# Attention in a gated block: sinks as a 129th score column, scaled queries, another order of transposes, stores and value loads

## The chip, the core and the metric

The kernel runs on one core of a Trainium2 chip. The metric is the device time of one execution in microseconds (us). Five engines work in parallel, each through its own instructions in their written order: TensorE (PE, with its weight loads PEld), VectorE (DVE), ScalarE (ACT), GpSimd (POOL) and SyncE (SP), which here issues all the DMAs.

## The reference

For 2048 positions of 1024 channels the block takes an RMS norm h, multiplies it by one wide weight (7680 columns), and feeds a convolution branch and an attention branch, which gates merge:

```python
proj = einsum("bsd,de->bse", h, w_in)          # glu_in, conv_gate, q, k, v, attn_gate, merge_logits
c = silu(layernorm(conv31(a * sigmoid(b)) + b_dw))
y_conv = (c * silu(conv_gate)) @ w_conv_out
# attention: 16 query heads, 4 key heads, head 64, window 128, rope on q and k
scores = where(mask, q k^T * 64 ** -0.5, -1e30)
m = maximum(max(scores), sink)
p = exp(scores - m)
probs = p / (sum(p) + exp(sink - m))
y_attn = ((probs v) * silu(attn_gate)) @ w_attn_out
merged = sigmoid(g_conv) * y_conv + sigmoid(g_attn) * y_attn
out = rmsnorm(x + merged @ w_out)
```

## The kernel before

Two sweeps of 1024 positions each run the same program. Every large product is made of three matmuls (high by high, high by low, low by high), since each operand is split into a rounded high half and what is left, its low half. Names begin `whi_` and `wlo_` for the halves of weights; in the first sweep POOL computes the low halves (L254) and SP stores them (L285), in the second sweep SP loads them again (L271). A projection (`project`, L297) is 48 matmuls of 512 columns into two of three PSUM banks "mm".

The order on PE is the order in which the program is written, and that comes from a planner, the class `Line`: it adds up PE's time (`spend`), and hands out the steps of side chains when they are due. `late` holds chains with a due time (`after`, `start`), `bg` the convolution's operations one per `every` us, `soon` one operation per step. The other engines' instructions are put in order ahead of time by dependences, estimated times and a priority (`tc.high_priority`).

The convolution is 31 taps for each of eight channel groups, each tap one pass of DVE over 1024 columns (L518). Attention runs beside the projections of the gates (`ag`, `cg`, `ma`, `mc`). It has 32 units a sweep, one per key head and block of 128 positions, ATT_EVERY = 13.8 us apart. A unit (`attention`, L720) is a chain of three steps with the pauses LAT between them:

- the scores `sc`, eight matmuls into two PSUM banks (L735); ACT copies and DVE masks them into the tile `ss` (L745, L748); DVE takes the maximum (L752), scales it and compares it with the negated sink (L753), and forms sink minus maximum (L755); ACT takes its exponential (L756) and those of the four heads with their sums (L758); DVE adds the sink's term (L760) and inverts (L761); ACT scales the rows (L763).
- four transposes of `ss` into one bank `tpp` (L768); ACT and DVE split it into `pt` (L775, L776), POOL selects from that `pc` (L780); the gate `ga` is loaded into `ss` (L771).
- six matmuls into the bank `ov` (L791); ACT and DVE add its two halves into `ss` (L797, L798), DVE multiplies by `ga` (L799), ACT and DVE split the product (L801, L802), and SP stores it to `d_a` (L804).

`sc`, `tpp` and `ov` share three PSUM banks, the pool "tp", in turn. Queries and keys of the next unit are loaded from DRAM (`qk`, L711, L715) when a unit begins, value tiles (`va`, `vb`, `vm`) per key head, eight units at once, when the last unit of a head has issued its product (`load_v`, L676). ACT changes its table of functions between the exponentials and the gates' functions (ACT_TABLE_LOAD). Gates are stored from their evacuation (L561), queries when two of a head's parts are split (L622). When all 32 units are stored, the output is loaded again as `aT` (L897) for the product `ya`.

## Time and profile before

| what | value |
|---|---|
| time, median of 3 runs (lowest, highest) | 2062.93 us (2062.31, 2063.85) |
| the profiled execution, time of its own | 2065.01 us |
| span from its first to its last instruction | 2063.3 us |
| mean granted TensorE clock in it | 0.991 |
| attention, first to last score matmul | 210.3 to 1698.3 us, in two sweeps |
| first and last load of `aT` in the first sweep | 645.9, 714.06 us |
| first `ya` matmul of the first and of the second sweep | 766.4, 1795.4 us |
| mean of one: ACT's Exp (L758), scaling (L763), copy of ov (L797), gate (L560) | 392, 393, 368, 600 ns |

The profile is of one execution. Its page has the busy time of each engine, the chain of work that ended last and the costliest groups of instructions by line; other views give the waits (which engine and line stood idle for whom, in all, how often, the longest), the timeline, and the busy time with the granted clock in chosen windows. A line such as L758 is a line of the kernel before.

### The profile page before, as it was taken

How to read it: one execution, taken by the hardware profiler on the slowest of the kernel's cores; microseconds unless marked ns; L12 is line 12 of the kernel's file. 1: busy time of each engine (PE TensorE's matmuls, PEld its weight loads, DVE VectorE, ACT ScalarE, POOL GpSimd, SP SyncE). 2: the span in 40 equal slices, each digit the busy share in tenths (PEclk: the TensorE clock that was granted, in tenths of full speed). 3: DMA queues.
4: the chain of work that ended last, by engine and by line, in shares of the span. 5: the costliest groups of instructions: out<-in, count | busy, mean ns of one | idle time of the engine just before them, and what ended most of it. 6: DMA issues, size and time to landing. Idle time of an engine off the chain costs nothing.

```text
span 2063.3 us, 27786 instructions
## 1 busy us (share of the span) xinstructions
PE 2001.2 (97%) x9264; PEld 1660.7 (80%) x9264; DVE 1330.4 (64%) x1930; ACT 1014.6 (49%) x2263; POOL 417.3 (20%) x398
## 2 busy tenths in 40 slices
PE   8999999999999999999999999999989999999998
PEld 7888788787887878888888778877878788888887
DVE  7998769888995266123766848589878934441224
ACT  8322576677657453124513125766666675621222
POOL 1454233233323322340001121111011110000200
PEclk9999999999999999999999999999999999999999
DMA  8656646546467857346646555565565668574432
GB/s 308 204 167 197 206 152 191 179 159 182 158 175 226 261 197 240 134 151 215 224 150 204 163 168 169 160 178 188 162 185 175 178 219 275 166 244 148 146 119 82
DMA packets 302015, 382.02 MB, mean 185 GB/s; under 512 B 29232, under 2 KB 160176, under 8 KB 301872
## 3 DMA queue, kind: packets, MB, share of 16 engines
q1 hardware_dynamic: 301872, 380.25, 58.1%
q8 instruction: 74, 1.21, 0.2%
q14 instruction: 69, 0.57, 0.1%
HBM read 252.20 MB, written 127.93 MB: 184 GB/s over the span
## 4 chain that ended last, share of the span: by engine, by line
PE 56%; DVE 20%; ACT 8%; DMA 3%; issue 2%; SPq 1%; POOL 0%; ACTq 0%; DVEq 0%; POOLq 0%
DVE acc L518 12%; PE o L1105 8%; PE mm_ya L292 8%; PE mm_yc L292 8%; PE mm_mc L292 7%; PE mm_ma L292 6%; PE mm_ga L292 4%; PE mm_gb L292 3%; PE mm_q_b L292 2%; PE mm_q_a L292 2%; ACT ss L758 2%; PE mm_cg L292 2%; DVE ss L798 1%; DVE st L752 1%; ACT L758 1%
## 5 line engine op out<-in xcount | busy, mean ns | idle before, releaser
L518 DVE SCALAR_TENSOR_TENSOR acc<-glu,par,acc 128x1024 f32<-128x1024 f32 x464 | 595.4, 1283 | 4.2
L780 POOL TENSOR_SCALAR_AFFINE_SELECT pc<-pt 64x512 fp32r<-64x512 f32 x128 | 83.6, 653 | 552.9 <-ACT pt L775 522.1
L1105 PE MATMUL o<-wo,mT 128*128 128x512 f32 x768 | 174.8, 389 | 0.0
L1105 PEld LDWEIGHTS o<-wo,mT 128*128 128x128 f32 x768 | 144.1, 188 | 30.0
L292 PE MATMUL mm_ma<-hT,whi_ma 128*128 128x512 f32 x512 | 162.7, 399 | 0.0
L292 PE MATMUL mm_cg<-hT,whi_cg 128*128 128x512 f32 x512 | 161.8, 397 | 0.0
L292 PE MATMUL mm_mc<-hT,whi_mc 128*128 128x512 f32 x512 | 158.4, 391 | 1.6 <-ACT mc L560 1.6
L292 PE MATMUL mm_ag<-hT,whi_ag 128*128 128x512 f32 x512 | 159.8, 393 | 0.0
L292 PE MATMUL mm_ya<-aT,whi_ya 128*128 128x512 f32 x512 | 157.7, 389 | 0.0
L292 PE MATMUL mm_yc<-uT,whi_yc 128*128 128x512 f32 x512 | 157.5, 389 | 0.0
L758 ACT ACT_TABLE_LOAD x57 | 73.1, 1283 | 142.0 <-DVE st L753 142.0
L292 PE MATMUL mm_ga<-hT,whi_ga 128*128 128x512 f32 x448 | 142.8, 400 | 0.0
L292 PE MATMUL mm_gb<-hT,whi_gb 128*128 128x512 f32 x448 | 139.9, 393 | 0.0
L292 PEld LDWEIGHTS mm_mc<-hT,whi_mc 128*128 128x128 f32 x512 | 95.3, 188 | 21.4 <-ACT mc L560 2.0
L292 PEld LDWEIGHTS mm_yc<-uT,whi_yc 128*128 128x128 f32 x512 | 96.1, 188 | 19.9
L292 PEld LDWEIGHTS mm_ya<-aT,whi_ya 128*128 128x128 f32 x512 | 96.0, 188 | 19.9
L292 PEld LDWEIGHTS mm_ma<-hT,whi_ma 128*128 128x128 f32 x512 | 94.8, 192 | 17.7
L798 DVE TENSOR_TENSOR ss<-ov,ss 64x256 f32<-64x256 f32 x128 | 53.7, 419 | 85.9 <-ACT ss L797 84.2
L292 PEld LDWEIGHTS mm_cg<-hT,whi_cg 128*128 128x128 f32 x512 | 94.0, 191 | 17.3
L292 PEld LDWEIGHTS mm_ag<-hT,whi_ag 128*128 128x128 f32 x512 | 93.4, 188 | 17.6
L292 PE MATMUL mm_ma<-hT,wlo_ma 128*128 128x512 f32 x256 | 101.7, 397 | 4.5 <-DMA wlo_ma<-d_lo 4.5
L292 PE MATMUL mm_cg<-hT,wlo_cg 128*128 128x512 f32 x256 | 101.2, 395 | 4.1 <-DMA wlo_cg<-d_lo 4.1
(450 smaller groups left out, 4350.8 us busy)
## 6 DMA issues: line engine op xcount, KB each, us to landing
qk<-d_q SPq DMA_DIRECT2D x256, 64.0 KB, 2.4
d_a<-ss SPq DMA_DIRECT2D x128, 128.0 KB, 2.2
aT<-d_a SPq DMA_DIRECT2D x32, 512.0 KB, 5.8
qk<-d_k SPq DMA_DIRECT2D x240, 64.0 KB, 2.0
d_q<-hq_c SPq DMA_DIRECT2D x16, 512.0 KB, 5.8
raw_ag<-in_w_in_dram SPq DMA_DIRECT2D x32, 256.0 KB, 3.2
d_ag<-ag SPq DMA_DIRECT2D x32, 256.0 KB, 2.2
ss<-d_ag SPq DMA_DIRECT2D x64, 128.0 KB, 2.5
```

Of the source, the lines that this page charges most:

```text
L292: pe.matmul(out=ps, lhsT=a, rhs=b, start=(k == 0 and i == 0), stop=(k == KC - 1 and i == 2))
L518: dve.scalar_tensor_tensor(out=to, in0=glu[c][:, j:j + T], scalar=tap(c, j), in1=acc[c], op0=ALU.mult, op1=ALU.add)
L752: dve.tensor_reduce(out=mx, in_=sb, axis=AX.X, op=ALU.max, negate=True)
L758: act.activation(out=sb[:, h, :], in_=sb[:, h, :], func=AF.Exp, scale=SCALE, bias=ngm[:, h:h + 1], accum_out=den[:, h:h + 1])
L780: pool.affine_select(out=pc[at], in_=f(pt[0:HD, a]), pattern=[[0, 2 * GQ], [1, HD]], compare_op=ALU.is_ge, fill=0.0, base=0, channel_multi ...
L798: dve.tensor_tensor(out=to, in0=ovp[own, :, r], in1=to, op=ALU.add)
L1105: pe.matmul(out=ps, lhsT=a[:, c0:c0 + P], rhs=r, start=(k == 0 and i == 0), stop=(k == KC - 1 and i == 2))
```

## The change

The query's split now applies the factor 1/8 (SCALE). The sink is copied by POOL into a 129th column beside each head's 128 scores, so that the maximum and the sum of exponentials run over 129 columns; the four small rows for the sink go. The pauses LAT become 27 and 7 us. A priority `front` is put on the evacuations of scores, transposes and ov. The gate `ga` moves from `ss` to the tile of `pc`. The stores of gates, queries and attention's output are handed to the planner for a later step. Value tiles are loaded in halves of four units into two places, two ahead; the first loads of attention come 10 us after its start.

```diff
-LAT = (19.0, 16.0)
+LAT = (27.0, 7.0)
...
-        dve.tensor_scalar(out=nsink, in0=sink_bc, scalar1=-1.0, scalar2=None, op0=ALU.mult)
...
+
+    def front():
+        return tc.high_priority(offset=20 * PRIO)
...
                 act.activation(out=g, in_=ps, func=func)
-                nc.sync.dma_start(out=spill[kind][s * KC + e, :, half * TH:(half + 1) * TH], in_=g)
-                if half == 1:
-                    stored.add((kind, e))
+
+                def store():
+                    nc.sync.dma_start(out=spill[kind][s * KC + e, :, half * TH:(half + 1) * TH], in_=g)
+                    if half == 1:
+                        stored.add((kind, e))
+
+                line.soon.append(store)
...
+        def drain():
+            while pend:
+                pend.popleft()()
+                yield 0.0, 2.0
+
+        def flush():
+            while pend:
+                pend.popleft()()
...
-                act.copy(hi, src)
-                split_lo(lo, src, hi, dve)
+                act.activation(out=hi, in_=src, func=AF.Copy, scale=SCALE)
+                dve.scalar_tensor_tensor(out=lo, in0=src, scalar=SCALE, in1=f(hi), op0=ALU.mult,
+                                         op1=ALU.subtract)
                 if r % 2:
                     b0 = s * 2 * NB + NB * half
+                    idle = not pend
                     for a in range(2):
-                        nc.sync.dma_start(out=d_q[a, i, :, b0:b0 + NB, r // 2, :],
-                                          in_=f(pair[n][a]).rearrange("p b h t -> p b (h t)"))
+                        pend.append(lambda a=a: nc.sync.dma_start(
+                            out=d_q[a, i, :, b0:b0 + NB, r // 2, :],
+                            in_=f(pair[n][a]).rearrange("p b h t -> p b (h t)")))
+                    if idle:
+                        line.start(drain())
...
+        def load_v(n):
+
+            g, b0 = n // 2, s * NB + 4 * (n % 2)
+            mix, da, db = (t[:, n % 2] for t in vg[0])
...
+            load(mix[low, n0:], high, 0, slice(b0 + n0 - 1, b0 + 3))
+            blk = slice(b0, b0 + 4)
+            load(mix[high], low, 0, blk)
+            for at in (low, high):
+                load(da[at], low, 1, blk)
+                load(db[at], high, 1, blk)
...
+        def reload(n):
+            load_v(n)
+            return
+            yield
+
+        def prepare_attention():
+            flush()
+            load_qk(0)
+            vg[0] = [slot(X[i], [P, 2, 4, P], F32R, f"v{'mab'[i]}{s}") for i in range(3)]
+            for n in range(2):
+                load_v(n)
+            return
+            yield
...
             ss = slot(next_of("ss", AT[4:7] + AT[13:14]), [P, 1024], F32, f"ss{u}")
-            sb = ss[:, 0:512].rearrange("p (h q) -> p h q", q=P)
-            oT, ga = (ss[:, c:c + 256].rearrange("p (a q) -> p a q", q=P) for c in (512, 768))
+            sx = ss[:, 0:4 * (P + 4)].rearrange("p (h q) -> p h q", q=P + 4)
+            sb, ext = sx[:, :, 0:P], sx[:, :, 0:P + 1]
+            oT = ss[:, 768:1024].rearrange("p (a q) -> p a q", q=P)
+            pool.tensor_copy(out=sx[:, :, P], in_=sink_bc[:, g * GQ:(g + 1) * GQ])
             if first:
...
-            dve.tensor_reduce(out=mx, in_=sb, axis=AX.X, op=ALU.max, negate=True)
-            dve.scalar_tensor_tensor(out=ngm, in0=mx, scalar=SCALE, in1=nsink[:, hd], op0=ALU.mult,
-                                     op1=ALU.min)
-            dve.tensor_tensor(out=dlt, in0=sink_bc[:, hd], in1=ngm, op=ALU.add)
-            act.activation(out=es, in_=dlt, func=AF.Exp)
+            with front():
+                for qh, sc in enumerate(scs):
+                    part = sb[:, 2 * qh:2 * qh + 2, :]
+                    if not first:
+                        act.copy(part, sc[:, :, 0:P])
+                    elif qh:
+                        act.copy(part[:, :, HD:], sc[:, :, HD:P])
+                    dve.copy_predicated(out=part[:, :, 0:HD], mask=tri_i, data=sc[:, :, P:3 * HD])
+            st = work.tile([P, 3, GQ], F32, tag="st", name=f"st{u}", bufs=4)
+            ngm, den, rinv = (st[:, i, :] for i in range(3))
+            dve.tensor_reduce(out=ngm, in_=ext, axis=AX.X, op=ALU.max, negate=True)
             for h in range(GQ):
-                act.activation(out=sb[:, h, :], in_=sb[:, h, :], func=AF.Exp, scale=SCALE,
-                               bias=ngm[:, h:h + 1], accum_out=den[:, h:h + 1])
-            dve.tensor_tensor(out=den, in0=den, in1=es, op=ALU.add)
+                act.activation(out=ext[:, h, :], in_=ext[:, h, :], func=AF.Exp, bias=ngm[:, h:h + 1],
+                               accum_out=den[:, h:h + 1])
             dve.reciprocal(out=rinv, in_=den)
             for h in range(GQ):
                 act.activation(out=sb[:, h, :], in_=sb[:, h, :], func=AF.Copy, scale=rinv[:, h:h + 1])
...
+            pcg = slot(next_of("pc", AT[9:11]), [P, 1024], F32R, f"pc{u}")
+            pc, ga = pcg[:, 0:TH], f(pcg[:, TH:TH + 2 * P]).rearrange("p (a q) -> p a q", q=P)
             nc.sync.dma_start(out=ga, in_=spill["ag"][e2, :, qs].rearrange("c p q -> p c q"))
             pt = slot(next_of("pt", AT[7:9]), [P, 2, TH], F32R, f"pt{u}")
             flat = tpp.rearrange("p h q -> p (h q)")
-            with tc.high_priority(offset=4 * PRIO):
+            with front():
                 act.copy(pt[:, 0], flat)
                 split_lo(pt[:, 1], flat, pt[:, 0], dve)
...
-            if b == NB - 1 and g + 1 < NKV:
-                load_v(g + 1)
+            if n % 4 == 3 and n // 4 + 2 < 2 * NKV:
+                line.after(4.0, reload(n // 4 + 2), lambda: True)
             ovp = ov.rearrange("p (q i r t) -> p i r q t", q=2, i=2, r=2)
-            for r, own, other in ((0, slice(0, HD), slice(HD, P)), (1, slice(HD, P), slice(0, HD))):
-                to = oT[own].rearrange("p i (q t) -> p i q t", t=HD)
-                act.copy(to, ovp[other, :, r])
-                dve.tensor_tensor(out=to, in0=ovp[own, :, r], in1=to, op=ALU.add)
+            rows = ((slice(0, HD), slice(HD, P)), (slice(HD, P), slice(0, HD)))
+            to = [oT[own].rearrange("p i (q t) -> p i q t", t=HD) for own, _ in rows]
+            with front():
+                for r in range(2):
+                    act.copy(to[r], ovp[rows[r][1], :, r])
+                for r in range(2):
+                    dve.tensor_tensor(out=to[r], in0=ovp[rows[r][0], :, r], in1=to[r], op=ALU.add)
             dve.tensor_tensor(out=oT, in0=oT, in1=ga, op=ALU.mult)
             hl = sb.rearrange("p (l c) q -> p l c q", c=2)
             act.copy(hl[:, 0].bitcast(F32R), oT)
             split_lo(hl[:, 1].bitcast(F32R), oT, hl[:, 0], dve)
-            for i in range(2):
-                nc.sync.dma_start(out=d_a[e2, :, i, qs].rearrange("c p q -> p c q"), in_=hl[:, i])
-            done[n] = True
...
-            yield 0.72, 0.0
+            yield 0.72, 4.0
+
+            def store():
+                for i in range(2):
+                    nc.sync.dma_start(out=d_a[e2, :, i, qs].rearrange("c p q -> p c q"), in_=hl[:, i])
+                done[n] = True
+
+            line.soon.append(store)
...
-            load_qk(0)
-            load_v(0)
+            line.after(10.0, prepare_attention(), lambda: True)
             for n in range(NKV * NB):
                 line.after(22.0 + n * ATT_EVERY, attention(n),
-                           lambda n=n: n not in begun or ("ag", 2 * (n // NB) + 1) in stored)
+                           lambda n=n: (n > 0 or 0 in qk or 0 in begun) and (n not in begun or ("ag", 2 * (n // NB) + 1) in stored))
```

Left out above are the pool sizes and slices that follow from these lines.

**One unit of attention.** On ACT, of the kernel before, from the copies of the scores of unit 0_1_4 (sweep, head, block) on; `cg` is a gate of the projections:

```order
L745 COPY ss0_1_4_3622<-sc0_1_4_0_3612 128x256
L745 COPY ss0_1_4_3622<-sc0_1_4_1_3617 128x256
L801 CAST ss0_1_1_3161<-ss0_1_1_3161 128x256
L758 ACT_TABLE_LOAD
L758 ACTIVATE ss0_1_4_3622,st0_1_4_3627<-ss0_1_4_3622,st0_1_4_3627 128x128
L756 ACTIVATE st0_1_4_3627<-st0_1_4_3627 128x4
L758 ACTIVATE ss0_1_4_3622,st0_1_4_3627<-ss0_1_4_3622,st0_1_4_3627 128x128 x2
L775 CAST pt0_1_3_3681<-tpp0_1_3_3675 128x512
L758 ACTIVATE ss0_1_4_3622,st0_1_4_3627<-ss0_1_4_3622,st0_1_4_3627 128x128
L560 ACT_TABLE_LOAD
L560 ACTIVATE cg0_1_0_3665<-mm_cg0_10_3595 128x512
```

On ACT, of the change, at the same place:

```order
L779 COPY ss0_1_4_3584<-sc0_1_4_0_3574 128x2x128
L779 COPY ss0_1_4_3584<-sc0_1_4_1_3579 128x2x128
L805 CAST pt0_1_2_3608<-tpp0_1_2_3601 128x512
L787 ACT_TABLE_LOAD
L787 ACTIVATE ss0_1_4_3584,st0_1_4_3590<-ss0_1_4_3584,st0_1_4_3590 128x129 x4
L562 ACT_TABLE_LOAD
L562 ACTIVATE cg0_1_0_3633<-mm_cg0_10_3552 128x512
L791 ACTIVATE ss0_1_4_3584<-ss0_1_4_3584,st0_1_4_3590 128x128 x2
L828 COPY ss0_1_2_3285<-ov0_1_2_3658 64x256 x2
```

The cast of `pt` stood behind three exponentials of the next unit and belonged to the unit one earlier; now it stands ahead of the table load, belongs to the unit two earlier, and the exponentials follow each other.

On DVE, of the kernel before, from the masked copies of the scores of unit 0_1_3 on; `acc` are taps of the convolution:

```order
L748 COPY_PREDICATED ss0_1_3_3476<-tri_96,sc0_1_3_0_3466 128x2x64
L518 SCALAR_TENSOR_TENSOR acc0_4_3660<-glu0_4_3244,par_81,acc0_4_3660 128x1024
L748 COPY_PREDICATED ss0_1_3_3476<-tri_96,sc0_1_3_1_3471 128x2x64
L518 SCALAR_TENSOR_TENSOR acc0_4_3660<-glu0_4_3244,par_81,acc0_4_3660 128x1024
L752 TENSOR_REDUCE st0_1_3_3481<-ss0_1_3_3476 128x4
L518 SCALAR_TENSOR_TENSOR acc0_4_3660<-glu0_4_3244,par_81,acc0_4_3660 128x1024
L753 SCALAR_TENSOR_TENSOR st0_1_3_3481<-st0_1_3_3481,nsink_103 128x4
L518 SCALAR_TENSOR_TENSOR acc0_4_3660<-glu0_4_3244,par_81,acc0_4_3660 128x1024
L755 TENSOR_TENSOR st0_1_3_3481<-sink_bc_102,st0_1_3_3481 128x4
L518 SCALAR_TENSOR_TENSOR acc0_4_3660<-glu0_4_3244,par_81,acc0_4_3660 128x1024
L254 TENSOR_TENSOR pt0_1_2_3533<-tpp0_1_2_3527,pt0_1_2_3533 128x512
L518 SCALAR_TENSOR_TENSOR acc0_4_3660<-glu0_4_3244,par_81,acc0_4_3660 128x1024 x2
```

On DVE, of the change, from the masked copies of unit 0_1_4 on:

```order
L782 COPY_PREDICATED ss0_1_4_3584<-tri_96,sc0_1_4_0_3574 128x2x64
L782 COPY_PREDICATED ss0_1_4_3584<-tri_96,sc0_1_4_1_3579 128x2x64
L520 SCALAR_TENSOR_TENSOR acc0_4_3628<-glu0_4_3212,par_81,acc0_4_3628 128x1024
L253 TENSOR_TENSOR pt0_1_2_3608<-tpp0_1_2_3601,pt0_1_2_3608 128x512
L785 TENSOR_REDUCE st0_1_4_3590<-ss0_1_4_3584 128x4
L520 SCALAR_TENSOR_TENSOR acc0_4_3628<-glu0_4_3212,par_81,acc0_4_3628 128x1024 x3
L789 RECIPROCAL st0_1_4_3590<-st0_1_4_3590 128x4
L520 SCALAR_TENSOR_TENSOR acc0_4_3628<-glu0_4_3212,par_81,acc0_4_3628 128x1024 x2
L830 TENSOR_TENSOR ss0_1_2_3285<-ov0_1_2_3658,ss0_1_2_3285 64x256 x2
L520 SCALAR_TENSOR_TENSOR acc0_4_3628<-glu0_4_3212,par_81,acc0_4_3628 128x1024
L831 TENSOR_TENSOR ss0_1_2_3285<-ss0_1_2_3285,pc0_1_2_3606 128x256
```

The low half of `pt` moved ahead of the maximum, the small rows at L753, L755 and L760 are gone, and both adds on `ov` stand together behind the reciprocal.

**Low halves of weights in the second sweep.** On SP, of the kernel before, around the weights of the projection `cg1_5` (sweep, column tile); `d_a` is the store of an attention unit, 1_2_0 the first of head 2:

```order
L711 DMA qk1_20_13578<-d_q_110 32x512 x4
L715 DMA qk1_20_13578<-d_k_111 32x2x256 x4
L804 DMA d_a_112<-ss1_2_0_13154 128x2x128 x2
L271 DMA wlo_cg1_50_13504<-d_lo_117 128x512
L271 DMA wlo_cg1_51_13510<-d_lo_117 128x512
L771 DMA ss1_2_3_13597<-d_ag_106 128x2x128
L268 DMA raw_cg1_61_13644<-in_w_in_dram 128x512
```

On SP, of the change, at the same place:

```order
L732 DMA qk1_20_13439<-d_k_110 32x2x256 x4
L270 DMA wlo_cg1_50_13376<-d_lo_116 128x512
L270 DMA wlo_cg1_51_13382<-d_lo_116 128x512
L267 DMA raw_cg1_60_13507<-in_w_in_dram 128x512
L267 DMA raw_cg1_61_13513<-in_w_in_dram 128x512
L267 DMA raw_cg1_70_13645<-in_w_in_dram 128x512
L267 DMA raw_cg1_71_13651<-in_w_in_dram 128x512
L801 DMA pc1_2_2_13620<-d_ag_105 128x2x128
L842 DMA d_a_111<-ss1_2_0_13024 128x2x128 x2
```

The loads of `wlo_cg1_5` moved ahead of the store of unit 1_2_0. On SP, of the kernel before, around the weights of `ma1_3`; `d_ma` are stores of gates (sweep, tile, half):

```order
L561 DMA d_ma_108<-ma1_1_1_14585 128x512
L711 DMA qk1_28_14754<-d_q_110 32x512 x4
L715 DMA qk1_28_14754<-d_k_111 32x2x256 x4
L561 DMA d_ma_108<-ma1_2_0_14666 128x512
L271 DMA wlo_ma1_30_14590<-d_lo_117 128x512
L271 DMA wlo_ma1_31_14596<-d_lo_117 128x512
```

On SP, of the change, at the same place:

```order
L707 DMA vb1_10662<-d_v_112 64x4x128
L801 DMA pc1_3_1_14638<-d_ag_105 128x2x128
L565 DMA d_ma_107<-ma1_1_1_14418 128x512
L270 DMA wlo_ma1_31_14430<-d_lo_116 128x512
L728 DMA qk1_28_14597<-d_q_109 32x512 x4
L732 DMA qk1_28_14597<-d_k_110 32x2x256 x4
L842 DMA d_a_111<-ss1_2_7_14033 128x2x128 x2
L270 DMA wlo_ma1_40_14567<-d_lo_116 128x512
L565 DMA d_ma_107<-ma1_2_0_14517 128x512
```

The pair of `wlo_ma1_3` stood behind the store of the gate `ma1_2_0`; its second load now stands ahead of it, and its first load some rows earlier.

**The start of attention in the second sweep.** On SP, of the kernel before, behind the last stores of queries:

```order
L622 DMA d_q_110<-hq1_2_3_a10_10501 128x8x128
L622 DMA d_q_110<-hq1_2_3_c5_10502 128x8x128
L271 DMA wlo_ga1_20_10670<-d_lo_117 128x512
L271 DMA wlo_ga1_21_10676<-d_lo_117 128x512
L711 DMA qk1_0_10680<-d_q_110 32x512 x4
L715 DMA qk1_0_10680<-d_k_111 32x2x256 x3
```

On SP, of the change:

```order
L640 DMA d_q_109<-hq1_2_3_a10_10418 128x8x128
L640 DMA d_q_109<-hq1_2_3_c5_10419 128x8x128
L728 DMA qk1_0_10651<-d_q_109 32x512 x4
L732 DMA qk1_0_10651<-d_k_110 32x2x256 x3
L270 DMA wlo_ga1_20_10583<-d_lo_116 128x512
L270 DMA wlo_ga1_21_10589<-d_lo_116 128x512
```

The seven loads of the first unit's queries and keys moved ahead of `wlo_ga1_2`; the stores of queries stand where they stood.

More of the change, by code (lines that the diff above doesn't have):

```diff
@@ L133, in hybrid_block @@
     sink_bc = const.tile([P, NH], F32, name="sink_bc")
-    nsink = const.tile([P, NH], F32, name="nsink")
     def load_sinks():
@@ L214, in finish_bg @@
         def finish_bg(self):
-            while self.bg:
-                self.bg.popleft()()
+            for ops in (self.soon, self.bg):
+                while ops:
+                    ops.popleft()()
         def finish(self):
@@ L673, in v_of, with load @@
             return vt[b // 2][:, b % 2, g, :]
-        def load_v(g):
-            mix, da, db = (slot(X[n], [P, NB, P], F32R, f"v{'mab'[n]}{s}_{g}") for n in range(3))
-            vg[0] = (mix, da, db)
-            lo_rows, hi_rows = slice(0, HD), slice(HD, P)
-            b0 = s * NB
-            n0 = 1 if s == 0 else 0
-            if n0:
-                dve.memset(f(mix[lo_rows, 0]), 0.0)
-            def load(to, b, at, rows, kind):
-                nc.sync.dma_start(out=f(to[at, b:]), in_=rows_of(b0 + b, rows, kind, b))
-            def rows_of(blk, rows, kind, b):
-                return d_v[blk:blk + NB - b, rows, kind, g].rearrange("b p d -> p b d")
-            nc.sync.dma_start(out=f(mix[lo_rows, n0:]),
-                              in_=d_v[b0 + n0 - 1:b0 + NB - 1, hi_rows, 0, g].rearrange("b p d -> p b d"))
-            load(mix, 0, hi_rows, lo_rows, 0)
-            for at in (lo_rows, hi_rows):
-                load(da, 0, at, lo_rows, 1)
-                load(db, 0, at, hi_rows, 1)
+        def load_v(n):
+            g, b0 = n // 2, s * NB + 4 * (n % 2)
+            mix, da, db = (t[:, n % 2] for t in vg[0])
+            low, high = slice(0, HD), slice(HD, P)
+            n0 = 1 if b0 == 0 else 0
+            if n0:
+                dve.memset(f(mix[low, 0]), 0.0)
+            def load(to, rows, kind, blk):
+                nc.sync.dma_start(out=f(to), in_=d_v[blk, rows, kind, g].rearrange("b p d -> p b d"))
+            load(mix[low, n0:], high, 0, slice(b0 + n0 - 1, b0 + 3))
[4 more added lines that the diff above has]
+                load(db[at], high, 1, blk)
         done, qk = {}, {}
@@ L740, in attention @@
             if first:
                 pool.memset(sb, NEG)
-            for qh, sc in enumerate(scs):
-                part = sb[:, 2 * qh:2 * qh + 2, :]
-                if not first:
-                    act.copy(part, sc[:, :, 0:P])
-                elif qh:
-                    act.copy(part[:, :, HD:], sc[:, :, HD:P])
-                dve.copy_predicated(out=part[:, :, 0:HD], mask=tri_i, data=sc[:, :, P:3 * HD])
-            st = work.tile([P, 6, GQ], F32, tag="st", name=f"st{u}", bufs=4)
@@ L750, in attention @@
-            mx, ngm, es, den, rinv, dlt = (st[:, i, :] for i in range(6))
-            hd = slice(g * GQ, (g + 1) * GQ)
-            dve.tensor_reduce(out=mx, in_=sb, axis=AX.X, op=ALU.max, negate=True)
-            dve.scalar_tensor_tensor(out=ngm, in0=mx, scalar=SCALE, in1=nsink[:, hd], op0=ALU.mult,
-                                     op1=ALU.min)
-            dve.tensor_tensor(out=dlt, in0=sink_bc[:, hd], in1=ngm, op=ALU.add)
-            act.activation(out=es, in_=dlt, func=AF.Exp)
+            with front():
[6 more added lines that the diff above has]
+                    dve.copy_predicated(out=part[:, :, 0:HD], mask=tri_i, data=sc[:, :, P:3 * HD])
@@ L784, in attention @@
             ov = tp_ps.tile([P, TH], F32, tag="tp", name=f"ov{u}")
-            mix, da, db = (t[:, b, :] for t in vg[0])
+            mix, da, db = (t[:, n // 4 % 2, b % 4, :] for t in vg[0])
             for qh in range(2):
```

6 lines of the change are left out of this document (3 added, 3 removed).

## Prediction

> **What bounds the kernel now.** The page comes first: it says which engine is full, and through which engines the chain of work that ended last runs.
>
> ```profile
> span 2063.3 us, 27786 instructions
> ...
> PE 2001.2 (97%) x9264; PEld 1660.7 (80%) x9264; DVE 1330.4 (64%) x1930; ACT 1014.6 (49%) x2263; POOL 417.3 (20%) x398
> ...
> PE 56%; DVE 20%; ACT 8%; DMA 3%; issue 2%; SPq 1%; POOL 0%; ACTq 0%; DVEq 0%; POOLq 0%
> ```
>
> TensorE (PE) is busy for 2001.2 of 2063.3 us, and the change takes no matmul away. So what it can win is the 62 us in which PE is idle, and what a slow clock costs inside the busy time. That a fifth of the chain is VectorE (DVE) says that in places PE runs at DVE's pace. The waits of PE over the whole run (line, what it waited for; us in all, times, longest) name the places:
>
> ```profile
> PE sc L735 <- DVE pt L254: 19.6, 21, 2.2
> PE tpp L768 <- DVE ss L798: 6.6, 5, 2.2
> ...
> PE mm_ma L292 <- DMA wlo_ma<-d_lo: 4.5, 1, 4.5
> PE mm_ga L292 <- DMA wlo_ga<-d_lo: 4.4, 1, 4.4
> PE mm_cg L292 <- DMA wlo_cg<-d_lo: 4.1, 2, 3.2
> PE mm_q_b L292 <- DMA wlo_q_b<-d_lo: 4.0, 1, 4.0
> PE sc L735 <- DMA qk<-d_k: 2.7, 1, 2.7
> PE ov L791 <- DMA vb<-d_v: 2.2, 4, 1.1
> ```
>
> 26.2 us (19.6 and 6.6) are waits for one of the three PSUM banks "tp", 17.0 us are waits for low halves of weights in the second sweep, 4.9 us for attention's own loads. Behind some of the long ones the clock is low, as the view by windows shows (length; busy us of PE, PEld, DVE, ACT, POOL; granted clock; DMA share, GB/s):
>
> ```profile
> 208.00:216.00 8.00, 5.71 (x22) 4.73 (x23) 1.78 (x6) 3.29 (x11) 0.00 (x0) 0.79 0.70 202
> 543.00:550.00 7.00, 4.76 (x18) 3.95 (x17) 6.75 (x11) 6.80 (x20) 1.30 (x2) 0.76 0.45 148
> 618.00:625.00 7.00, 4.82 (x19) 4.00 (x18) 7.00 (x11) 5.90 (x14) 2.58 (x3) 0.76 0.61 198
> ...
> 1223.00:1233.00 10.00, 6.54 (x17) 5.15 (x18) 0.00 (x0) 0.00 (x0) 0.00 (x0) 0.66 0.69 193
> 1523.00:1533.00 10.00, 6.83 (x20) 5.12 (x20) 6.85 (x14) 6.58 (x20) 1.22 (x2) 0.66 0.69 195
> 1632.00:1642.00 10.00, 5.48 (x15) 4.05 (x15) 9.90 (x15) 8.43 (x21) 1.30 (x2) 0.66 0.46 148
> ```
>
> What is missing from clock 1 is time lost: 7 x 0.24 = 1.7 us in each of the two windows behind waits for a bank (543 and 618), 10 x 0.34 = 3.4 us in each of the three behind waits for weights, 8 x 0.21 = 1.7 us behind the first scores. The Trainium skill ("TensorE: Matmul & The Clock Gate", Part 1) says that the clock falls to half after an idle window of about 3.4 us; by that the bank waits, none over 2.2 us here, would cost no clock, and their clock term below would be 0 instead of 1.7 us. The windows at 543 and 618 us speak against it.
>
> **Why PE waits for a bank.** The timeline around one unit (start, length, engine, line, what; in brackets the idle time before it):
>
> ```profile
> 462.78 0.60 PE L768 MATMUL tpp<-ident_r,ss 128*128 128x128 f32 x4
> ...
> 468.33 1.28 ACT L758 ACT_TABLE_LOAD   x1 [3.81 <-DVE st L753]
> ...
> 469.63 0.40 ACT L758 ACTIVATE ss<-ss,st 128x128 f32<-128x128 f32 x1
> ...
> 470.03 0.57 ACT L775 CAST pt<-tpp 128x512 fp32r<-128x512 f32 x1
> ...
> 470.75 0.68 DVE L254 TENSOR_TENSOR pt<-tpp,pt 128x512 fp32r<-128x512 f32 x1
> ...
> 471.49 0.69 PE L735 MATMUL sc<-qk 128*128 128x192 f32 x4 [0.78 <-DVE pt L254]
> ```
>
> The transposes are done at 463.4, but their cast (L775) stands on ScalarE (ACT) behind the next unit's first Exp, whose table load waits 3.81 us for DVE's L753. So the bank comes free 8 us after it was filled, and the next scores wait for it.
>
> **Term 1, banks.** In the changed kernel the transposes follow right behind the scores of the unit two later, and on ACT their cast stands ahead of the Exps. The part that is late next is what DVE has to do before the bank of "ov" is free. Durations (line, engine, operation; busy us, mean ns of one):
>
> ```profile
> L518 DVE SCALAR_TENSOR_TENSOR acc<-glu,par,acc 128x1024 f32<-128x1024 f32 x464 | 595.4, 1283 | 4.2
> L798 DVE TENSOR_TENSOR ss<-ov,ss 64x256 f32<-64x256 f32 x128 | 53.7, 419 | 85.9 <-ACT ss L797 84.2
> L254 DVE TENSOR_TENSOR pt<-tpp,pt 128x512 fp32r<-128x512 f32 x64 | 43.9, 687 | 47.4 <-ACT pt L775 47.3
> L752 DVE TENSOR_REDUCE st<-ss 128x4 f32<-128x512 f32 x64 | 43.6, 681 | 0.9
> L748 DVE COPY_PREDICATED ss<-tri,sc 128x128 f32<-128x128 int32 x128 | 35.7, 298 | 19.4 <-PE sc L735 10.0 <-ACT ss L745 8.0 <-ACT ss L747 0.5
> ...
> L761 DVE RECIPROCAL st<-st 128x4 f32<-128x4 f32 x64 | 11.0, 172 | 0.9
> L745 ACT COPY ss<-sc 128x256 f32<-128x256 f32 x120 | 40.3, 372 | 5.7 <-PE sc L735 5.3
> ```
>
> In DVE's new order (shown with the change) a unit has, from its first masked copy on: 2 x 0.30, one tap 1.28, the low half of pt 0.69, the maximum 0.68, three taps 3.85, the reciprocal 0.17, two taps 2.57, both adds 2 x 0.42: 10.7 us. It begins 1.0 us after the scores do (four of them 0.6, ACT's copy 0.37), so the adds end at 11.7. The next transposes stand at 13.8 (the pitch of units) + 0.9 (their scores) = 14.7: 3.0 us in hand. ACT keeps up: from the maximum to the adds it has two table loads (2.6 us), four Exps (1.6), and a gate, two scalings and two copies at 0.3 to 0.6 (2.0), 6.2 us beside DVE's 6.6.
>
> With the unit's other rows (three taps, 1.0 us of small ones) DVE needs 15.6 us for 13.8 of PE. So it falls behind by 1.8 us a unit while a channel's 31 taps last (9 a unit, some 3.4 units) and catches up afterwards: the third and fourth unit of each stretch would wait, 0.6 and 1.8 us, and twelve stretches make 29 us. But the same working for the order of before (ten taps and three small rows more, 17.0 us a unit; 4.5 us in hand until the scores) gives 68 us where 26.2 are measured. Scaled by that ratio it is 11 us, and 28 us with ten taps a unit, as some units have. **I take half of the 26.2 as gone, 13.1 us**, and half of the clock behind them, 1.7 us. The ends are all 29.6 us gone, and nothing gained or worse (rival 2). The product "ov" itself, 7 us behind the transposes instead of 16, needs pt's low half, which is there at 1.0 + 0.6 + 1.3 + 0.7 = 3.6 us, with ov at 8.3: that cover of 4.7 us hides it, and each us by which it is missed would cost up to 64.
>
> **Term 2, weights behind stores.** SyncE (SP) issues in order. Its rows ahead of the waits at 1527 and 1637 us, and its longest wait:
>
> ```profile
> 1523.17 0.99 SPq L804 DMA_DIRECT2D d_a<-ss  x2
> ...
> 1524.26 0.92 SPq L271 DMA_DIRECT2D wlo_cg<-d_lo  x2
> ...
> 1633.40 0.34 SPq L561 DMA_DIRECT2D d_ma<-ma  x1
> ...
> 1633.79 0.97 SPq L271 DMA_DIRECT2D wlo_ma<-d_lo  x2
> SPq L804 <- ACT ss L745: 63.9, 32, 7.3
> ```
>
> The first time SP stands 7.3 us at the store of an attention unit that isn't computed yet, the second time at a gate's store. In the new order the loads of both stand ahead of the store that held them. I count both waits as gone: 3.2 + 4.5, with their clock 2 x 3.4, **14.5 us** (ends 0, and 15.4 with the smaller wait of mm_cg).
>
> **Term 3, value tiles.** They come in halves of four units, loaded some 55 us before their use (four units): the 2.2 us of waits go. There are 96 loads instead of 48. Six load-issues more in eight units, 3 us if each takes as long as a query load below, are hidden while SP only waits; where it doesn't, what stands behind them comes 3 us later.
>
> **Term 4, the starts of attention.**
>
> ```profile
> 201.69 2.00 SPq L561 DMA_DIRECT2D d_ag<-ag  x1
> ...
> 1223.26 2.04 SPq L711 DMA_DIRECT2D qk<-d_q  x4
> 1225.35 1.39 SPq L715 DMA_DIRECT2D qk<-d_k  x3
> ```
>
> In the first sweep the gate's store no longer stands ahead of the first query loads: 2.0 of the 2.7 + 1.7 us go. In the second sweep the order turns against the change: wlo_ga, for which PE waits 4.4 us, now stands behind those seven loads, 2.04 + 1.39 = **3.4 us lost** (ends 0, and 6 with the time of their data). The wait for wlo_q_b stays, since the query stores ahead of it stand where they stood.
>
> **Costed at nothing:** the 129th column (the small rows that fall away with it are in term 1; three ns more for each Exp), a POOL copy of four sinks a unit (POOL is busy 20%), the scale in the split (the same tile read once, as before). Attention's last store comes some us later in program order, and its readers over 40 us behind that.
>
> **Sum.** 13.1 + 1.7 + 14.5 + 2.2 + 2.0 - 3.4 = 30.1 us off the profiled execution's 2065.0 (the span and 1.7 around it): 2034.9. That execution lay 2.1 us above the median of 2062.93, so **2033 us** for a median.
>
> **Rivals.** (1) More: the lag never comes to 3.0 us, and all waits for banks and for the first scores go, 14.8 + 2.4 us more: 2016. For it speaks that three small rows of DVE and one of ACT, each behind the other engine, leave every unit; against it the dense taps. (2) Slower: transposes waiting for the adds on ov take the place of the waits removed, since from ov to the next transposes there are 6.4 us now and were 11. The other terms win 15.3 us and the banks at most 29.6, so it decides from 44.9 / 64 = 0.7 us a unit; at 1 us in all 64 units the time is 2063 - 45 + 64 = 2082. A rule of the Trainium skill ("ScalarE: Activation LUTs", What ACT_TABLE_LOAD costs) leads there: 2.66 us for each switch of tables, with a drain, would put ACT's copies of ov 2.8 us later and use up what is in hand. The trace has 1.30 us from the load's start at 468.33 to the Exp at 469.63, so I don't count with it. (3) Same: weights still come late behind other rows of SP, and DVE sets the pace as before; terms 1 and 2 fall away, 2062.
>
> **Chances.** Forecast 0.60, rival 1 0.15, rival 2 0.13, rival 3 0.12. The forecast's own range is 2022 to 2048 (half of the bank terms more or all of them kept). For 8 in 10 the range takes in rival 1 and half of rival 3: 2013 to 2062. A measurement of this kernel can tell about 0.2%, 4 us, from no change: faster 0.60 + 0.15 + 0.03 of rival 3 = 0.78, same 0.10 (most of rival 3, some of 2), slower 0.12.
>
> **What would show it.** In the waits of PE: "sc <- DVE pt" nearly gone and "tpp <- DVE" at 10 to 15 us (right), under 3 (rival 1) or over 45 (rival 2). No wait for wlo_cg or wlo_ma over 2 us, about 8 us for wlo_ga, none for vb. The clock under 1 only at the starts of attention and for wlo_q_b. ACT's cast of pt within 2 us of the transposes. Wrong would be a new wait of ov for pt or pc, or weights late behind the value loads.

## The result and the profile after

The changed kernel takes 2038.88 us (median of 4 runs, 2035.34 to 2039.75); the kernel before, run beside it, 2062.62 (2062.31 to 2063.85). The ratio is 0.9881, with a 95% interval of 0.9863 to 0.9898: faster by 1.2%. The profiled execution took 2039.39 us, its span is 2037.7 us, its mean granted clock 0.995 (0.991 before).

The page of the changed kernel, busy us of each engine, share of the span and number of instructions:

```profile
span 2037.7 us, 27935 instructions
...
PE 1989.0 (98%) x9264; PEld 1658.1 (81%) x9264; DVE 1312.7 (64%) x1737; ACT 1002.2 (49%) x2193; POOL 431.0 (21%) x462
```

The span is 25.6 us shorter. PE is idle for 48.7 us instead of 62.1 (13.4 less) and busy for 12.2 us less with as many matmuls. Of those 12.2 about 8 are clock (0.004 of the span); the other 4, a slightly quicker pace of the matmuls, were not followed further.

What PE waited for in the changed kernel (engine, tile and line; us in all, times, longest):

```profile
PE tpp L796 <- DVE ss L830: 19.7, 21, 3.1
PE ov L820 <- POOL pc L809: 7.9, 7, 2.2
PE mm_gb L291 <- ACT u_c L361: 5.5, 1, 5.5
PE mm_ga L291 <- DMA wlo_ga<-d_lo: 5.4, 1, 5.4
PE tpp L796 <- ACT ss L791: 1.1, 2, 0.8
PE mm_q_b L291 <- DMA wlo_q_b<-d_lo: 0.8, 1, 0.8
PE ov L820 <- DVE pt L253: 0.6, 1, 0.6
```

L796 is the transposes, L830 the adds on ov, L820 the product ov, L809 POOL's selects that write pc. The scores no longer wait for a bank (19.6 us before), but the transposes wait 19.7 us for theirs, and ov waits 8.5 us, mostly for pc: a wait that did not exist. The weights that cost 17.0 us cost 6.2.

What holds pc is seen in the timeline of the changed kernel (start, duration, engine, line, operation, tiles; in brackets the idle time before it):

```profile
417.06 2.39 POOL L527 TENSOR_TENSOR csum<-csum,cv 128x1024 f32<-128x1024 f32 x1 [2.94 <-DVE cv L520]
417.10 0.68 DVE L253 TENSOR_TENSOR pt<-tpp,pt 128x512 fp32r<-128x512 f32 x1
...
419.39 1.37 POOL L809 TENSOR_SCALAR_AFFINE_SELECT pc<-pt 64x512 fp32r<-64x512 f32 x2
...
420.82 0.39 PE L820 MATMUL ov<-pc,va 128*128 128x256 f32 x1 [1.79 <-POOL pc L809]
```

DVE has pt's low half ready at 417.78. POOL issues in order and is in the middle of the convolution's channel sum (L527), so the selects start at 419.39 and ov 1.8 us late.

### The profile page after: what moved, and what is told of

Same layout as the page of the kernel before. It is cut to its first block, busy times and chain, and to the rows that moved or that the text cites. A ratio compares the mean times of both kernels' runs of the same rounds, so it can differ in the third digit from the quotient of the medians.

```text
span 2037.7 us, 27935 instructions
## 1 busy us (share of the span) xinstructions
PE 1989.0 (98%) x9264; PEld 1658.1 (81%) x9264; DVE 1312.7 (64%) x1737; ACT 1002.2 (49%) x2193; POOL 431.0 (21%) x462
## 4 chain that ended last, share of the span: by engine, by line
PE 56%; DVE 20%; ACT 6%; issue 5%; DMA 2%; POOL 2%; SPq 1%; POOLq 0%; ACTq 0%; DVEq 0%
DVE acc L520 12%; PE o L1140 9%; PE mm_yc L291 9%; PE mm_mc L291 8%; PE mm_ya L291 7%; PE mm_ga L291 6%; PE mm_ma L291 5%; PE mm_gb L291 3%; PE mm_cg L291 2%; PE mm_ag L291 1%; ACT ss L787 1%; DVE st L785 1%; PE mm_q_a L291 1%; PE mm_v L291 1%; ACT L787 1%
## 5 line engine op out<-in xcount | busy, mean ns | idle before, releaser
L809 POOL TENSOR_SCALAR_AFFINE_SELECT pc<-pt 64x512 fp32r<-64x512 f32 x128 | 84.5, 660 | 272.1 <-ACT pt L805 229.8
L830 DVE TENSOR_TENSOR ss<-ov,ss 64x256 f32<-64x256 f32 x128 | 53.8, 420 | 116.0 <-ACT ss L828 114.5
L787 ACT ACTIVATE ss<-ss,st 128x129 f32<-128x129 f32 x256 | 100.2, 394 | 16.9 <-DVE st L785 16.1
```

The lines of the kernel that those rows point to most:

```text
L787: act.activation(out=ext[:, h, :], in_=ext[:, h, :], func=AF.Exp, bias=ngm[:, h:h + 1], accum_out=den[:, h:h + 1])
L809: pool.affine_select(out=pc[at], in_=f(pt[0:HD, a]), pattern=[[0, 2 * GQ], [1, HD]], compare_op=ALU.is_ge, fill=0.0, base=0, channel_multi ...
L830: dve.tensor_tensor(out=to[r], in0=ovp[rows[r][0], :, r], in1=to[r], op=ALU.add)
```

## The experiments

Twelve kernels ran, each beside the kernel before (whose medians were 2063.4 to 2064.8 us in those three groups), so they are compared by ratio. "Banks" is what PE waited in the profiled execution for DVE to empty a bank of "tp", "ov" what ov waited for pc or pt, "weights" all waits for low halves, "idle" the span less PE's busy time.

| kernel | median, us | ratio to before, 95% | banks | ov | weights | PE idle |
|---|---|---|---|---|---|---|
| before | 2062.6 | 1 | 26.4 | 0 | 17.0 | 62.1 |
| changed | 2038.9 | 0.9881 (0.9863 to 0.9898) | 19.7 | 8.5 | 6.2 | 48.7 |
| order_back | 2030.9 | 0.9837 (0.9822 to 0.9851) | 19.1 | 0 | 6.2 | 39.6 |
| stores_now | 2039.1 | 0.9883 (0.9868 to 0.9897) | 19.8 | 8.9 | 6.9 | 50.5 |
| half_taps | 2002.6 | 0.9700 (0.9685 to 0.9714) | 1.0 | 3.6 | 4.5 | 21.8 |
| no_csum | 2030.6 | 0.9834 (0.9817 to 0.9850) | 19.3 | 2.6 | 4.6 | 42.6 |
| front_back | 2046.5 | 0.9920 (0.9905 to 0.9934) | 35.9 | 0 | 6.5 | 55.9 |
| value_back | 2040.0 | 0.9888 (0.9873 to 0.9903) | 18.8 | 9.1 | 6.7 | 51.7 |
| sinks_back | 2065.9 | 1.0014 (1.0004 to 1.0024) | 23.4 | 2.7 | 10.8 | 63.8 |
| lat_16_16 | 2027.6 | 0.9824 (0.9809 to 0.9839) | 14.8 | 0 | 8.4 | 37.4 |
| sinks_only | 2036.6 | 0.9872 (0.9857 to 0.9887) | 19.0 | 0 | 9.8 | 42.6 |
| stores_only | 2061.1 | 0.9984 (0.9974 to 0.9993) | 28.9 | 0 | 8.4 | 58.1 |
| lat_17_18 | 2030.0 | 0.9837 (0.9823 to 0.9852) | 18.7 | 0 | 6.6 | 41.7 |
| lat_17_18_pool | 2011.7 | 0.9748 (0.9733 to 0.9762) | 6.2 | 0 | 6.2 | 26.4 |

### The order: order_back

```
-LAT = (27.0, 7.0)
+LAT = (19.0, 16.0)
```

> The changed kernel with the two delays of an attention unit set back (transposes 19 us behind their scores and the product ov 16 us behind those, instead of 27 and 7); all else of the change stays. Theory A (the new order took some waits for banks away and made as many others): the waits of PE "tpp <- DVE ss" (19.7 us in the changed kernel) fall below 5 us and "ov <- POOL pc" (7.9 us) vanishes, while "sc <- DVE pt" comes back with 15 to 22 us; the time stays within 5 us of the changed kernel's 2038.9, 2034 to 2044. Theory B (the order brings what the prediction gave it, 14.8 us, and the rest of the change brought less): 2049 to 2056, with sc <- DVE pt above 25 us. Theory C (the new order costs time on balance): under 2033.

2030.94 us: the waits are theory A's, the time is theory C's, under 2033. Its waits of PE begin:

```profile
PE sc L766 <- DVE pt L253: 19.1, 15, 3.3
```

The waits of the transposes and of ov are gone, and the bank waits stand at the scores again, as large as in the changed kernel. The new order moved them and added the 8.5 us of ov: with the other parts in place it costs 8 us. It also costs DVE time: DVE is busy for 1300.7 us here and for 1312.7 in the changed kernel, with the same instructions. Most of that is the low half of the attention product (L253 on `ss`), which takes 515 ns in the mean here and 654 there; the last section shows why.

### The stores: stores_now and stores_only

stores_now issues every store at once, in the changed kernel; stores_only holds back the stores of gates and of attention's output in the kernel before. Of the edit of stores_now:

```
 def ev(half, ps):
     g = t2k(f"{kind}{s}_{e}_{half}")
     act.activation(out=g, in_=ps, func=func)
...
-    line.soon.append(store)
+    store()
```

> The changed kernel with every store issued where its data is made in the program (gates, queries, attention units), none held back. Theory A (the deferral alone brings the weights early): PE waits again 3 to 5 us each for wlo_cg and wlo_ma, wlo_q_b goes from 0.8 back to about 4, the first scores wait 2 us or more for qk, and the clock is halved for 6.8 us behind two or three of them; 15 to 22 us lost, 2054 to 2061. Theory B (these loads come early because the attention steps stand elsewhere in SyncE's order, so the deferral counts for little): no wait for weights over 2 us beside wlo_ga's 5.4, 2037 to 2043.

2039.13 us and no wait for wlo_cg or wlo_ma: theory B. Held stores bring the changed kernel nothing.

> The kernel before with the gates' and attention's stores issued later, as in the change, and nothing else. Theory A (term 2 as the prediction had it: weights stand behind stores that aren't ready): no wait for wlo_cg and wlo_ma above 1 us, their two stretches of half clock gone, 2046 to 2053. Theory B (the stores' place isn't what makes these two loads late): waits of 3 us and more for two weights, 2059 to 2065.

2061.14 us, ratio 0.9984 (0.9974 to 0.9993): a gain of some 3 us. Both theories are half right: the waits for wlo_cg and wlo_ma are gone, and the time is theory B's. The timeline of the kernel before, and then that of stores_only, at this place (rows of PE with an idle time before them):

```profile
1637.65 0.79 PE L292 MATMUL mm_ma<-hT,wlo_ma 128*128 128x512 f32 x1 [4.52 <-DMA wlo_ma<-d_lo]
```

```profile
1634.19 0.69 PE L740 MATMUL sc<-qk 128*128 128x192 f32 x4 [0.60 <-DVE pt L255]
1652.07 0.95 PE L740 MATMUL sc<-qk 128*128 128x192 f32 x4 [3.93 <-DVE pt L255]
```

PE no longer stands 4.52 us for the weight, but it then stands 3.93 us at the scores for a bank that is not empty. Why the bank is late is seen on the other engines of stores_only:

```profile
1643.33 2.44 POOL L526 TENSOR_TENSOR csum<-csum,cv 128x1024 f32<-128x1024 f32 x1 [8.47 <-DVE cv L519]
...
1644.49 1.30 DVE L758 SCALAR_TENSOR_TENSOR st<-st,nsink 128x4 f32<-128x4 f32 x1
...
1645.86 1.28 ACT L763 ACT_TABLE_LOAD   x1 [3.36 <-DVE st L758]
...
1650.71 0.58 ACT L780 CAST pt<-tpp 128x512 fp32r<-128x512 f32 x1
...
1651.32 0.69 DVE L255 TENSOR_TENSOR pt<-tpp,pt 128x512 fp32r<-128x512 f32 x1 [2.01 <-ACT pt L780]
```

The small row of the sink (L758) lasts 1.30 us beside POOL's addition, ACT's Exps wait for it, and the cast of `pt`, which frees the bank, stands behind the Exps on ACT. This chain is hardly earlier than in the kernel before, where the same row ends at 1646.79 us (1645.79 here); PE, without its pause, reaches the scores 8 us earlier (1647.55 instead of 1655.76). DVE itself has gaps of 2.95 and 2.01 us there: its lag with the taps starts the chain late, and ACT carries it on.

Over the whole run the exchange is not one for one. The waits for weights fall by 8.6 us, those for banks rise by 2.5 us, other waits rise too, and PE is idle for 4.0 us less. The mean clock stays at 0.991.

### DVE's load: half_taps

```
 def nxt(j):
+    if j % 2 and j != 15:
+        return
     to = acc[c]
```

> The changed kernel without 14 of the convolution's 31 taps (the odd ones but the 15th are left out; what is computed is another convolution), with PE's order the same. Theory A (transposes wait because DVE is behind with taps when the adds on ov are due): "tpp <- DVE ss" falls from 19.7 us to under 3, the waits of ov for pc stay at 5 to 9 us, and the time falls by 17 to 24 us with the clock behind the waits, 2015 to 2022. Theory B (the adds are late because ACT copies ov late, behind table loads and gates): the waits for tpp stay above 12 us, and the time is 2030 to 2039.

2002.59 us, 1.0 us of bank waits: theory A, with 12 us more of gain than it asked for, and 3.6 us of waits for pc where it had 5 to 9.

```profile
PE mm_gb L291 <- ACT u_c L361: 5.6, 1, 5.6
PE mm_ga L291 <- DMA wlo_ga<-d_lo: 3.8, 1, 3.8
PE ov L822 <- POOL pc L811: 3.6, 3, 1.8
PE tpp L798 <- DVE ss L832: 1.0, 2, 0.6
```

With 14 of 31 taps away, 272 us of DVE's busy time, the same order of PE hardly waits for a bank. So the waits of the changed kernel come from DVE's backlog in the stretches dense with taps, not from ScalarE's (ACT's) copies alone.

### POOL's queue: no_csum

```
-    pool.tensor_tensor(out=conv_sum[0], in0=conv_sum[0], in1=cv[c], op=ALU.add)
+    pass
```

> The changed kernel without the additions of channels 1 to 7 to the convolution's channel sum on POOL (14 additions of 128 x 1024 left out, 2.4 us each; the mean of the layer norm is then that of one channel). Theory A (ov waits for pc because such an addition stands between or ahead of the two selects in POOL's order): "ov <- POOL pc" falls from 7.9 us to under 2 (what the sink copies cost stays), with at most one half-clock stretch less; the time falls by 6 to 9 us, 2030 to 2033. Theory B (the selects are late because DVE writes pt's low half late, and POOL is only the last to report): the waits stay at 5 to 8 us, some of them under "ov <- DVE pt", and the time stays at 2036 to 2040.

2030.57 us, 8.3 less than the changed kernel, with 2.6 us of waits for pc left: theory A, whose "under 2" is just missed. That is as much as undoing the order wins: what the new order costs stands at POOL's additions, and without them it brings no more than the old order has with them. The 8.3 us are not the wait for pc alone, since DVE is busy for 11.0 us less too (1301.7 instead of 1312.7). The old order without the additions was not run.

### Priorities and value tiles: front_back and value_back

front_back takes the two new `with front():` away and gives the transposes' copies `tc.high_priority(offset=4 * PRIO)` again.

> The changed kernel with the priorities of before: masked copies and copies of the scores and the four operations on ov no longer put in front, the two on the transposes in front by as much as before; each half of ov copied and added in turn. Theory A (putting them in front is what makes attention's stores ready early, so that SyncE no longer stands at them and the weights behind come early): PE waits again 3 to 5 us each for wlo_cg and wlo_ma, SyncE stands 7 us and more at a store of attention, and the waits for banks rise above 30 us; 2052 to 2066. Theory B (the order of the rows decides the banks, priorities little): waits for banks 18 to 26 us, no wait for weights beside wlo_ga, 2036 to 2045.

2046.49 us, above theory B's band and below A's. A is wrong in its mechanism (no wait for wlo_cg or wlo_ma) and right about the banks, 35.9 us. So putting the rows in front is worth 7.6 us: 16.2 us less at the banks, against the 8.5 us of ov, which doesn't wait for pc or pt here. Why it doesn't wasn't followed.

```
-if n % 4 == 3 and n // 4 + 2 < 2 * NKV:
-    line.after(4.0, reload(n // 4 + 2), lambda: True)
+if n % 8 == 7 and n // 4 + 2 < 2 * NKV:
+    for m in range(2):
+        load_v(n // 4 + 1 + m)
```

> The changed kernel with the value tiles of the next eight units loaded together (12 loads in a row behind the last product ov of a group), instead of four units at a time and four units ahead. Theory A (the waits for wlo_cg and wlo_ma of before came from that burst in SyncE's order): waits of 3 to 5 us for weights at one to three of the six changes of group, and 2 to 4 us in all for vb; with the clock 8 to 18 us lost, 2047 to 2057. Theory B (only the value tiles themselves come late): 2 to 4 us for vb and at most one stretch of half clock, 2040 to 2044. Theory C (hidden): under 2040.

2039.97 us, with no wait for vb: theory C, by a hair in the time, since theory B begins at 2040. The interval of its ratio overlaps that of the changed kernel: no effect can be told.

### The 129th column: sinks_back and sinks_only

sinks_back puts the small rows back into the changed kernel; the scaling in the queries' split stays. sinks_only puts the column into the kernel before, with that scaling and with the gate's tile beside `pc`, and nothing else. Of the edit of sinks_back:

```
-dve.tensor_reduce(out=ngm, in_=ext, axis=AX.X, op=ALU.max, negate=True)
+dve.tensor_reduce(out=mx, in_=sb, axis=AX.X, op=ALU.max, negate=True)
+dve.tensor_tensor(out=ngm, in0=mx, in1=nsink[:, hd], op=ALU.min)
+dve.tensor_tensor(out=dlt, in0=sink_bc[:, hd], in1=ngm, op=ALU.add)
+act.activation(out=es, in_=dlt, func=AF.Exp)
...
+dve.tensor_tensor(out=den, in0=den, in1=es, op=ALU.add)
```

> The changed kernel without the 129th column: the minimum with the negative sink, the difference, its Exp and the addition to the sum are back (three small rows of DVE and one of ACT in each unit), and POOL's copy of four sinks is gone. Theory A (those rows stand in the chain that makes DVE late in dense stretches): "tpp <- DVE ss" rises from 19.7 to 24 to 32 us, "ov <- POOL pc" falls by 0.5 to 2 us as the copies that wait for a store leave POOL; 2042 to 2050. Theory B (small rows fall into idle time, POOL's copy was the only one that mattered): waits for tpp 18 to 22 us, 2035 to 2040.

2065.9 us: theory A in direction, 16 us beyond its band. All that the change had won is gone. PE is idle for 15.1 us more than in the changed kernel and busy for 11.4 us more, at a mean clock of 0.987 instead of 0.995: more than a third of the loss isn't waiting, but slower matmuls.

> The kernel before with one part of the change alone: the sink as a 129th column, copied in by POOL, with the queries scaled in their split (the gate's tile moves beside pc to make room); order, stores, value tiles and priorities of before. Theory A (the three small rows of DVE and the one of ACT that leave each unit are worth some 25 us in any order, since each waits its turn behind taps): 2036 to 2046, "sc <- DVE pt" well under 19.6 us. Theory B (they are only worth that in the new order, which needs the transposes' input sooner): 2055 to 2063, with waits for banks 20 to 27 us. In both, the waits for wlo_cg and wlo_ma stay if nothing but the stores' place makes them.

2036.63 us, ratio 0.9872 (0.9857 to 0.9887): theory A. This part alone is worth as much as the whole change (0.9863 to 0.9898). The bank waits, 19.0 us, are not "well under 19.6", though: theory A is right about the time. Its waits of PE:

```profile
PE sc L734 <- DVE pt L252: 19.0, 15, 3.1
PE mm_gb L290 <- ACT u_c L357: 5.7, 1, 5.7
PE mm_cg L290 <- DMA wlo_cg<-d_lo: 3.7, 2, 2.7
PE mm_ma L290 <- DMA wlo_ma<-d_lo: 3.1, 1, 3.1
PE mm_q_b L290 <- DMA wlo_q_b<-d_lo: 2.1, 1, 2.1
PE mm_ga L290 <- DMA wlo_ga<-d_lo: 0.9, 1, 0.9
```

What the column takes off DVE is read from the rows on the small tile `st`, of the kernel before and then of sinks_back (operation, count: shortest, median and longest in ns, first and last start in us):

```profile
L753 DVE SCALAR_TENSOR_TENSOR st<-st,nsink x64: 148/158/1322, 212.8 to 1700.1; 128x4 f32<-128x4 f32 x64
L755 DVE TENSOR_TENSOR st<-sink_bc,st x64: 152/157/572, 213.0 to 1700.3; 128x4 f32<-128x4 f32 x64
L760 DVE TENSOR_TENSOR st<-st x64: 152/161/1816, 214.8 to 1703.4; 128x4 f32<-128x4 f32 x64
```

```profile
L787 DVE TENSOR_TENSOR st<-st,nsink x64: 147/155/1331, 210.9 to 1701.0; 128x4 f32<-128x4 f32 x64
L793 DVE TENSOR_TENSOR st<-st x64: 152/163/1979, 212.9 to 1704.3; 128x4 f32<-128x4 f32 x64
```

By their medians the three rows of before are 64 x (0.158 + 0.157 + 0.161) = 30.5 us of DVE. Single ones last up to eleven times as long, so that their busy time is 42.5 us (13.9, 10.5 and 18.1). Each stands between a row of DVE and one of ACT, so a late one makes the Exps, or the scalings and with them the transposes, late as well: in sinks_back the transposes also wait 12.8 us for ACT's scalings (1.1 in the changed kernel).

That the column brings the gain is shown from both sides. How is shown in part: PE is idle for 19.5 us less in sinks_only than before, of which the banks are 7.4 us, waits for weights 7.2 and attention's own loads 4.1; PE is also busy for 9.5 us less. Why loads come sooner was not found.

### Time in hand or load: lat_16_16, lat_17_18 and lat_17_18_pool

The first two only set `LAT` to (16.5, 16.0) and (17.0, 18.0). The third has also:

```
-split_lo(hl[:, 1].bitcast(F32R), oT, hl[:, 0], dve)
+split_lo(hl[:, 1].bitcast(F32R), oT, hl[:, 0], pool)
```

> The changed kernel with the transposes 16.5 us behind their scores (some 3.6 us behind the next unit's) and ov 16 us behind those: between the order of the change (right behind, 7) and that of order_back (some 6 us behind, 16). Theory A (waits for banks come from too little time between two rows of PE, and here the least, from the transposes to the scores that need their bank, is 10 us instead of 7.7 in order_back): "sc <- DVE pt" falls from order_back's 19.1 us to under 9, no wait of ov for pc, waits of tpp for DVE under 5: 2016 to 2024. Theory B (DVE is behind by more than any of these times in the dense stretches, and a move only changes the row at which PE waits): waits for banks 14 to 24 us in all, 2026 to 2034.

> The changed kernel with the transposes 17 us behind their scores (about 4 us behind the next unit's) and ov 18 us behind those (about 8 to 9 us behind the scores two units later): each of the three banks' waits then has 8 to 10 us in hand (lat_16_16: 6 for ov on the copies of the scores; order_back: 7.7 for the scores on pt). Theory A (the least of the three times in hand decides): waits for banks under 10 us in all, 2017 to 2025. Theory B (DVE's lag is larger than any of them): 13 to 20 us, 2025 to 2032.

2027.58 and 2029.96 us, 14.8 and 18.7 us of bank waits: theory B both times. The waits stood at ov in the first, the row with the least in hand by its reckoning (6 us), and mostly at the transposes in the second. They shrank by a quarter of order_back's 19.1 at most.

> lat_17_18 with the low half of the attention product split on POOL instead of DVE (0.42 us a unit off DVE). Theory A (DVE's work in the dense stretches sets the waits for banks): a third to a half of lat_17_18's bank waits go, 2 to 7 us less than it. Theory B (DVE and POOL disturb each other, or the stores that POOL now feeds come later and hold SyncE): within 2 us of lat_17_18, or slower.

2011.74 us, 18.2 less than lat_17_18: theory A in kind, at more than twice its size. Its waits of PE:

```profile
PE mm_gb L291 <- ACT u_c L361: 5.7, 1, 5.7
PE mm_ga L291 <- DMA wlo_ga<-d_lo: 4.5, 1, 4.5
PE tpp L796 <- DVE ss L830: 3.5, 4, 2.1
PE sc L766 <- DVE pt L253: 1.8, 2, 1.4
```

Moving 0.42 us a unit (64 x 0.42 = 27 us by the median; DVE is busy for 30.3 us less, POOL for 47.5 more) takes away two thirds of the bank waits, where moving PE's rows about took a quarter at most. At 0.9748 (0.9733 to 0.9762) this is the fastest kernel of the study that leaves nothing out, 27 us below the changed one.

## Why the prediction came out as it did

**The total** held: 2038.9 against 2033, inside the forecast's own 2022 to 2048. The sum behind it did not hold term by term: its two largest terms were given to parts that brought little or nothing, and a part costed at nothing brought the gain. That the total came close is in large part luck.

**Term 1, banks (14.8 us): the step that failed.** "I take half of the 26.2 as gone" put the gain down to the new order and sized it by the time in hand between rows of PE. Measured, the banks fell by 6.7 us (26.4 to 19.7): the scores' waits went as foreseen, but the transposes' rose to 19.7 us where 10 to 15 were foreseen. With the other parts in place the order brought nothing and cost 8 us, at ov and in DVE's time; alone, in the kernel before, it was not run. What helped the banks was in the change but not in that step: the column (7.4 us of banks in sinks_only) and the rows put in front (16.2 us of banks, 7.6 in all).

**"That cover of 4.7 us hides it"** was the second error in this term. It followed pt's low half on DVE, which was there in time (0.6 us of waits), and left out the queue of POOL behind it. The text named a wait of ov for pc as what would prove it wrong, and that came: 7.9 us. Taking POOL's additions away won 8.3 us (no_csum).

**Term 2, weights (14.5 us).** The two waits are gone, as foretold, and stores_only shows that holding the stores does that in the order of before. But the kernel got some 3 us for it there and nothing in the changed kernel: the step that failed is "I count both waits as gone", taken as time. In stores_only PE came sooner to banks that DVE and ACT had not freed sooner. The clock part (6.8 us of the term) shows the same: the slow stretches behind the two weights are gone from stores_only, but its mean clock is still 0.991, with new ones behind bank waits of 2 to 4 us. In the changed kernel the mean clock did rise, to 0.995, and three slow stretches lie behind waits of the transposes (338 and 617 us) and of ov (1423 us), where the forecast's list of signs had none. Why stores_now doesn't wait for these weights either stays open. In sinks_only, where stores are issued at once too, the waits are there (3.7 and 3.1 us), so it is the order, the priorities or the loads' new places that keep them away; no run tells which.

**Term 3, value tiles (2.2 us).** The waits are gone, but they stay gone in value_back, so with the other parts in place the halves aren't needed for it. In sinks_only, with the old loads, 0.5 us of them are left.

**Term 4, first scores.** All of the 2.7 us went (2.0 foreseen), wlo_ga lost 1.0 us instead of 3.4, and wlo_q_b, which "stays", fell from 4.0 to 0.8. It is at 4.0 again in sinks_back. How the column, which works in attention only, reaches a load ahead of attention was not found.

**"Costed at nothing: the 129th column."** This is the largest miss: with the scaling that goes with it, 28 us alone (2064.8 to 2036.6 in one group). The rows were seen, but given to term 1 as "three small rows more" in the order of before, where they only helped to scale a wait; rival 1 named them as its reason. It is this part, more than any other, that makes the kernel faster.

**The rivals.** Rival 1's mechanism (small rows leaving DVE) was at work, without ending the waits. Rival 2's mechanism was there at 19.7 us over 64 units, 0.31 us a unit, under the 0.7 from which it decides. Rival 3's sentence that DVE sets the pace as before is true of both kernels.

## What to carry to other kernels

Where an engine falls behind in dense stretches, the waits that PE shows come from its backlog, and they move from row to row: removing one wait, or giving one row more time, mostly lets the next appear. Look first for what an edit takes off the engine that is behind, and off the chain of handoffs between engines. There is no fixed rate: here 27 us off DVE (lat_17_18_pool) bought 18, three rows of 0.16 us with their handoffs bought 28, and 272 us of taps (half_taps) bought 36. And when work is pulled forward, follow every queue on its path to its last row, POOL's included.
